# Residual blocks of the last stage in a tile of their own, a regrouped first half of the output projection, and two changed orders at the ends of a two-layer diffusion backbone

## Chip, cores and metric

One core of one Trainium2 chip runs the whole kernel. The metric is the device time of one execution in microseconds; the time of the kernel before is the median of three runs.

## The reference, cut to what matters

The reference is one step of a backbone with two layers on 640 tokens (128 of a prompt, 512 of a sample) of 1024 channels each. What the change touches is the start of the first layer and the second half of the second:

```
m = silu(cond) @ w_mod + b_mod;  shift, scale, gate = split(m, 3)      # both layers
h = rmsnorm(x, norm_g) * (1 + scale) + shift
proj = h @ w_in
...
# odd layer
c_out = b_c * conv3(c_c * x_c) * silu(g_c)
z = conv31(a_d * sigmoid(b_d)) + conv_d_b
z = silu(layernorm(z, ln_g, ln_b));  d_out = z * silu(g_d)
x = x + gate * (concat(c_out, d_out) @ w_out)
# after both layers
y = rmsnorm(x, final_g)
```

## The kernel before, in words

**Layout and arithmetic.** Activations are kept with the channels on the 128 partitions and the 640 tokens in the free dimension, as eight tiles of 128 channels. Every product of the projections is made of three matrix products: weights and activations are each split into a rounded part and the rest (`split`, L111: ScalarE casts the high part, VectorE subtracts for the low part), and hi*hi, hi*lo and lo*hi are added up in PSUM. A weight chunk is 128 by 1024. `dma_w` (L117) loads it into one of two `w_raw` buffers, `split_w` (L122) makes its `w_hi` and `w_lo`, of which there are four each.

**The start** (L264 to L422) is written out by hand: TensorE, ScalarE, VectorE and the DMA queue of SyncE (SP) run in the order of the code. SP loads the eight token tiles `x`, then chunks `wm` of the modulation weights (`load_mod`, L275, two chunks of 512 KB for each of the eight channel tiles, eleven buffers) and the first weight chunks `w_in[20]`, `w_in[21]`, `w_in[22]` (L288 to L291, L358). The third, `w_in[22]`, goes to the buffer that the first chunk has had, so its load waits until VectorE has read the first chunk. TensorE makes the modulation of channel tile d in `mod_rows(d)` (L318, 32 small products on both chunks of d, tile `modacc`), and with `mains(k, ...)` (L364) it multiplies the first three weight chunks with channel tile k as soon as that is normalised. `mains(0, (2,))` (L400) is the first that needs the third chunk.

**The middle** is ordered by the scheduler of the tile framework: the work of an engine is placed by its own estimates, and a pool of buffers that is closed gives its space to the next one, whose tiles then wait for the last use of the old ones. Pool `lp` holds the layer's residual `x2` (eight tiles) and, until the end, the helpers `sq_acc2`, `sq2` and `xr2` of the first layer's closing norm. Pool `lq`, opened at L799, holds what the second layer needs, among it `grow` and `frow`: the gate and the final norm's weights as rows on all partitions, which the SP queue loads there at L810 and L813.

**The last stage** turns the layout: the output projection of the second layer puts tokens on the partitions (five blocks c of 128 tokens) and the 1024 output channels in the free dimension, in two halves of 512 columns. The residual must be turned too. VectorE transposes `x2` in squares of 32 into `xb` (L934, eight transposes, held behind the layer norm by `behind`), and sixteen transfers on the SP queue gather it as `xt` (L937). `xb` and `xt` use the two buffers of tag `h`, which the activations `h_hi` and `h_lo` have held until the last gate's products (`gate_d(3)`, L912). For a finished block of a half, `finish_t` (L952) multiplies PSUM by the gate row into `ft` (L956, which frees the PSUM bank), adds `ft` to `xt` (L957), and squares and sums on ScalarE (L959). In the first half it does so block by block (L977 to L979). In the second half the root of the mean square follows, then the scaling of both halves (ScalarE the left, VectorE the right) and the store of the block.

TensorE's accumulators for the second half partly reuse the banks of the first. Its last 4 of 8 channel tiles go block by block (L993); the last block's columns go in two pieces of 256 (`last`).

Of the kernel before, what the change touches and what calls it, by code (L numbers as in the profile page):

```python
# [57 lines left out]
def build(nc, tc, ctx, a):  # L58
# [18 lines left out]
    def two(t, n):  # L77
        return t.rearrange("p (a b) -> p a b", b=n)
# [189 lines left out]
    with ExitStack() as st:  # L268
# [85 lines left out]
        mod_fin(0, rows)  # L354
        xr(0)
        first = [split_w(raws[0])]
        load_mod(2, 1)
        raws.append(dma_w(w_in[22], nc.sync))  # L358
        load_mod(2, 1)
        load_mod(3)  # L360
        load_mod(4)
        fps = [pmm.tile([P, 1024], F32, name="mm") for _ in range(2)]

# [352 lines left out]
        nc.sync.dma_start(t, a["xN"][:, m])  # L716
        return t

    accs = lp.tile([P, T], F32, name="sq_acc2", bufs=1)

    def finish(m, ps, res, hs_):
        g = mod[0][:, 2, m, :]
        out = x2[m]
        if len(hs_) == 2:
            segs = ((0, ps_prompt(ps), out[:, 256:384], res[:, 256:384]),
                    (1, ps_sample(ps), tok_sample(out), tok_sample(res)))
        elif hs_[0] == 0:
# [9 lines left out]
        sq = lp.tile([P, T], F32, name="sq2", tag="sq2")[:, t0:t1]  # L737
# [58 lines left out]
    GWD = TG + 2 * PADC  # L796
    fill_mod(99)
    modc.close()
    lq = ctx.enter_context(tc.tile_pool(name="lq", bufs=2))  # L799
    dr = ctx.enter_context(tc.tile_pool(name="dr", bufs=1, space=bass.MemoryType.DRAM))  # L800
    gcol = lq.tile([P, 2, SQ], F32, name="gcol", bufs=1)
    grow = lq.tile([P, 2, D], F32, name="grow", bufs=1)
    frow = lq.tile([P, D], F32, name="frow", bufs=1)
# [5 lines left out]
    for c in range(2):  # L809
        nc.sync.dma_start(two(grow[:, c, :], 256), bass.AP(  # L810
            tensor=gd_.tensor, offset=gd_.offset + 256 * c, ap=[[0, P], [SQ * SQ, 4], [1, 256]]))
    fg = a["final_g"]
    nc.sync.dma_start(frow, bass.AP(tensor=fg.tensor, offset=fg.offset, ap=[[0, P], [1, D]]))  # L813
# [100 lines left out]
    for t0, t1 in GH:  # L914
        stat = pst.tile([P, 512], F32, name="stat")
        rs = lp.tile([P, 96], F32, name="rs2")
        bc = pst.tile([P, 512], F32, name="bc")
        stat_add(stat, var[:, t0:t1], t1 - t0, ones, True, True)
        rsqrt_bcast(stat, rs, lambda g, w: bc[:, g * w:(g + 1) * w], t1 - t0, 2.0)
        for i in range(4):  # L920
            ln_last = V.tensor_tensor(cv[i][:, t0:t1], cv[i][:, t0:t1], bc[:, 0:t1 - t0], op=ALU.mult)
    for i in range(4):
        zd = lq.tile([P, TG], F32, name="zd", tag="tmp")
        S.activation(zd, cv[i], AF.Silu, bias=sm("ln_b")[:, i:i + 1], scale=sm("ln_g")[:, i:i + 1])
# [3 lines left out]
        put_o(4 + i, do)  # L928

    NB5 = T // P  # L930
    xb = hpool.tile([P, T // SQ, NK, SQ], F32, name="xb", tag="h", bufs=2)
    xt = hpool.tile([P, NB5, D], F32, name="xt", tag="h", bufs=2)
    for m in range(NK):
        behind(V.transpose(xb[:, :, m, :], two(x2[m], SQ)), ln_last)  # L934
    for q in range(4):
        for g in range(4):
            nc.sync.dma_start(  # L937
# [11 lines left out]
            if pin:  # L949
                tc.keep_in_program_order(op)  # L950

    def finish_t(c, ps, half, n0, n1, j):  # L952
        cond_ = 0 if c == 2 else 1
        cs = slice(512 * half + n0, 512 * half + n1)
        t = lq.tile([P, T], F32, name="ft", tag="tmp")[:, 0:n1 - n0]
        V.tensor_tensor(t, ps[:, n0:n1], grow[:, cond_, cs], op=ALU.mult)  # L956
        V.tensor_tensor(xt[:, c, cs], xt[:, c, cs], t, op=ALU.add)  # L957
        sj = lq.tile([P, 512], F32, name="sqj", tag="c3", bufs=1)
        S.activation(sj[:, 0:n1 - n0], xt[:, c, cs], AF.Square, scale=D ** -0.5, accum_out=sums[:, c, j:j + 1])  # L959
        if j == 0:  # L960
            V.tensor_scalar(sums[:, c, 3:4], sums[:, c, 0:1], EPS, None, op0=ALU.add)
        elif n1 < 512:
            V.tensor_tensor(sums[:, c, 3:4], sums[:, c, 3:4], sums[:, c, j:j + 1], op=ALU.add)
        else:
            S.activation(sums[:, c, j:j + 1], sums[:, c, j:j + 1], AF.Sqrt, bias=sums[:, c, 3:4])
            V.reciprocal(sums[:, c, j:j + 1], sums[:, c, j:j + 1])
            return sums[:, c, j:j + 1]
# [25 lines left out]
    for c in range(NB5):  # L993
        if c < NB5 - 1:
            for k in range(4, NK):
                mm_t(acc[c], ws[k // 2 - 2], c, k, 0, 512, False, k == NK - 1, True)
            r = finish_t(c, acc[c], 1, 0, 512, 1)
        else:
            for j, (ps, n0, n1) in enumerate(last):
                for k in range(4, NK):  # L1000
                    mm_t(ps, ws[k // 2 - 2], c, k, n0, n1, False, k == NK - 1, True)
                r = finish_t(c, ps, 1, n0, n1, 1 + j)
        S.activation(xt[:, c, 0:512], xt[:, c, 0:512], AF.Copy, scale=r)
        V.scalar_tensor_tensor(xt[:, c, 512:D], xt[:, c, 512:D], r, frow[:, 512:D], op0=ALU.mult, op1=ALU.mult)
        if c < NB5 - 1:
            nc.sync.dma_start(a["out_y"][:, c, :], xt[:, c, :])
        else:
            S.dma_start(a["out_y"][:, c, 0:512], xt[:, c, 0:512])
            nc.sync.dma_start(a["out_y"][:, c, 512:D], xt[:, c, 512:D])
# [82 lines left out]
```

## Time and profile before

| what | value |
|---|---|
| median of 3 runs | 592.65 us (592.51 to 593.09) |
| the profiled execution: its own time / its span | 594.55 us / 592.8 us |
| mean granted TensorE clock | 0.992 |
| TensorE matmul (PE) busy | 577.9 us, 97% of the span, 4032 instructions |
| VectorE (DVE) busy | 448.0 us, 76% |
| ScalarE (ACT) busy | 230.2 us, 39% |
| GpSimd (POOL) busy | 39.3 us, 7% |
| DMA | 78.41 MB, mean 132 GB/s |

The profile is of one execution. PE stands for TensorE's matmuls, PEld for its weight loads, DVE for VectorE, ACT for ScalarE, SPq and ACTq for the DMA issues of SyncE and ScalarE. A row of the timeline has the start and the duration in us, the engine, the line of the kernel, the operation, what is written and read, the shape, the count, and in brackets how long the engine sat idle before it and what ended the wait. A row of the stretches has the stretch, its length, busy time and count of PE, PEld, DVE, ACT and POOL, the granted clock, the DMA share and GB/s. A row of the waits says who waited for whom: us in total, times, longest.

### The profile page before, as it was taken

The page shows a single profiled execution, that of the slowest core. Times are in us where ns is not written, and L with a number is a line of the kernel's source. Part 1 is how long each engine was busy: PE and PEld are TensorE (multiplying, and loading weights), DVE is VectorE, ACT ScalarE, POOL GpSimd, SP SyncE. Part 2 cuts the span into 40 slices and gives each one's busy share as a digit, 9 for nine tenths or more (in the row PEclk, how much of TensorE's full clock was granted, in tenths as well). Part 3 has the DMA queues.
Part 4 walks back from the last instruction along what each step waited for, and adds up shares of the span by engine and source line. Part 5 has one row for each costly group of instructions (what it writes and reads, how often), then busy time and mean ns, then how long its engine had stood idle before and what let it go on. Part 6 is the DMA issues. An engine that isn't in the chain of part 4 may idle for free.

```text
span 592.8 us, 10089 instructions
## 1 busy us (share of the span) xinstructions
PE 577.9 (97%) x4032; PEld 527.4 (89%) x4032; DVE 448.0 (76%) x808; ACT 230.2 (39%) x413; POOL 39.3 (7%) x90
## 2 busy tenths in 40 slices
PE   9899999999999999999999999999999999999975
PEld 5689999988988787878999999999999999988764
DVE  0566577699879788765737989999999996369356
ACT  6457322223354555463425531123222222354135
POOL 1000000230005132200000000000000000000000
PEclk9899999999999999999999999999999999999988
DMA  8894666656824242410941232222222222122804
GB/s 315 341 383 139 177 185 174 163 172 228 268 83 145 83 140 76 138 58 28 330 124 37 72 107 72 95 81 76 71 72 72 72 72 74 68 72 65 184 0 179
DMA packets 27823, 78.41 MB, mean 132 GB/s; under 512 B 3200, under 2 KB 8960, under 8 KB 27648
## 3 DMA queue, kind: packets, MB, share of 16 engines
q1 hardware_dynamic: 18416, 43.94, 23.2%
q10 hardware_dynamic: 9360, 33.82, 16.9%
q8 instruction: 32, 0.52, 0.4%
q14 instruction: 15, 0.12, 0.1%
HBM read 71.96 MB, written 3.16 MB: 127 GB/s over the span
## 4 chain that ended last, share of the span: by engine, by line
PE 92%; DMA 3%; DVE 2%; SPq 1%; ACT 1%; issue 1%; POOL 0%; ACTq 0%; DVEq 0%; POOLq 0%
PE mm L162 68%; PE mm L947 5%; PE ps_o L616 3%; PE ps_s L586 3%; PE ps_t L604 3%; PE ps_s L531 2%; PE mm L300 2%; PE modacc L323 1%; DMA w_raw<-in_w_out_odd 1%; DMA wm<-in_w_mod 1%; PE ps_t L531 1%; PE ps_o L531 1%; PE mm L531 1%; SPq L937 1%; PE mm L493 1%; PE bc L200 1%
## 5 line engine op out<-in xcount | busy, mean ns | idle before, releaser
L162 PE MATMUL mm<-h_hi,w_hi 128*128 128x384 f32 (+1 forms) x768 | 181.8, 314 | 0.0
L162 PE MATMUL mm<-h_lo,w_hi 128*128 128x384 f32 (+1 forms) x768 | 181.1, 311 | 0.5 <-DVE h_lo L344 0.5
L162 PE MATMUL mm<-h_hi,w_lo 128*128 128x384 f32 (+1 forms) x768 | 181.2, 311 | 0.0
L112 ACT CAST w_hi<-w_raw 128x1024 fp32r<-128x1024 f32 x68 | 70.9, 1053 | 162.9 <-PE mm L162 132.0
L162 PEld LDWEIGHTS mm<-h_hi,w_hi 128*128 128x128 f32 x768 | 119.4, 189 | 3.5 <-issue 2.1
L162 PEld LDWEIGHTS mm<-h_lo,w_hi 128*128 128x128 f32 x768 | 119.7, 189 | 2.5 <-issue 1.4
L162 PEld LDWEIGHTS mm<-h_hi,w_lo 128*128 128x128 f32 x768 | 119.7, 188 | 1.1 <-issue 1.1
L893 DVE SCALAR_TENSOR_TENSOR cv<-gl,small,cv 128x656 f32<-128x656 f32 x120 | 101.4, 897 | 0.4
L115 DVE TENSOR_TENSOR w_lo<-w_raw,w_hi 128x1024 fp32r<-128x1024 f32 x68 | 83.5, 1229 | 20.2 <-ACT w_hi L112 20.0
L259 DVE SCALAR_TENSOR_TENSOR junk<-wt,condb 128x1024 bf16<-128x1024 f32 x64 | 78.7, 1229 | 4.2 <-DMA wt<-in_w_modT 3.3
L162 PE MATMUL mm<-o_lo,w_hi 128*128 128x384 f32 (+1 forms) x128 | 34.3, 314 | 0.0
L162 PE MATMUL mm<-o_hi,w_lo 128*128 128x256 f32 (+1 forms) x128 | 33.9, 312 | 0.0
L162 PE MATMUL mm<-o_hi,w_hi 128*128 128x384 f32 (+1 forms) x128 | 33.8, 312 | 0.0
L947 PE MATMUL mm<-w_hi,o_hi 128*128 128x512 f32 (+1 forms) x72 | 27.5, 382 | 3.7 <-DVE ft L956 3.7
L947 PE MATMUL mm<-w_lo,o_hi 128*128 128x512 f32 (+1 forms) x72 | 27.1, 376 | 0.0
L947 PE MATMUL mm<-w_hi,o_lo 128*128 128x512 f32 (+1 forms) x72 | 26.8, 372 | 0.0
L606 ACT COPY pt<-ps_t 128x384 f32<-128x384 f32 (+1 forms) x36 | 16.8, 466 | 24.3 <-PE ps_t L604 24.1
L595 ACT ACTIVATE sn<-sn,mx 128x384 f32<-128x384 f32 x32 | 19.6, 614 | 12.6 <-DVE mx L592 11.6
L162 PEld LDWEIGHTS mm<-o_hi,w_hi 128*128 128x128 f32 x128 | 21.6, 188 | 0.8 <-issue 0.6
L162 PEld LDWEIGHTS mm<-o_hi,w_lo 128*128 128x128 f32 x128 | 21.6, 189 | 0.5 <-issue 0.5
L162 PEld LDWEIGHTS mm<-o_lo,w_hi 128*128 128x128 f32 x128 | 21.6, 189 | 0.5 <-issue 0.3
L592 DVE CUSTOM_DVE_ANT_0 sn<-ps_s,bias 128x384 f32<-128x384 f32 x32 | 17.2, 552 | 5.4 <-PE ps_s L586 5.3
(228 smaller groups left out, 712.3 us busy)
## 6 DMA issues: line engine op xcount, KB each, us to landing
wt<-in_w_modT SPq DMA_DIRECT2D x32, 512.0 KB, 4.6
w_raw<-in_w_in_odd ACTq DMA_DIRECT2D x28, 512.0 KB, 4.0
wm<-in_w_mod SPq DMA_DIRECT2D x16, 512.0 KB, 8.1
w_raw<-in_w_in_even ACTq DMA_DIRECT2D x16, 512.0 KB, 3.8
w_raw<-in_w_out_even ACTq DMA_DIRECT2D x8, 512.0 KB
w_raw<-in_w_out_odd ACTq DMA_DIRECT2D x8, 512.0 KB, 4.0
x<-in_xT SPq DMA_DIRECT2D x8, 320.0 KB, 7.0
xre<-in_xN SPq DMA_DIRECT2D x8, 320.0 KB
```

The lines of the kernel that those rows point to most:

```text
L112: op = S.copy(hi, src)
L115: V.tensor_tensor(lo, src, hi.bitcast(F32), op=ALU.subtract)
L162: PE.matmul(ps[:, PB + t0:PB + t1], ww[:, ks], xx[k][:, t0:t1], start=(first and i == 0), stop=(last and i == 2))
L259: tc.keep_in_program_order(V.scalar_tensor_tensor(junk, wt, 1.0, condb[:, c, :], op0=ALU.mult, op1=ALU.mult, accum_out=mod[l][:, j, d, c:c ...
L531: PE.matmul(vps[c], xx[k][:, vsl[c]], ww, start=(k == 0 and n == 0), stop=(k == NK - 1 and n == 2))
L586: chain(PE.matmul(sps[hh][:, 0:384], qq[hr, qs], km, start=(n == 0), stop=(n == 2)))
L592: V.tensor_tensor_reduce(out=sn, in0=sps[:, 0:384], in1=bs[hh][b], scale=-1.0, scalar=3e38, op0=ALU.add, op1=ALU.min, accum_out=mx)
L595: S.activation(sn, sn, AF.Exp, bias=mx, scale=-1.0, accum_out=sume)
L604: chain(PE.transpose(tps[:, c * P:(c + 1) * P], sn[:, c * P:(c + 1) * P], ident))
L616: chain(PE.matmul(po[hr, b * P:(b + 1) * P], vv, pts[hh][:, n * P:(n + 1) * P], start=(n == 0), stop=(n == 2)))
L893: V.scalar_tensor_tensor(z, gl[i][:, w:w + TG], cd[:, i, w:w + 1], z, op0=ALU.mult, op1=ALU.add)
L947: op = PE.matmul(ps[:, n0:n1], xx[k][:, c * P:(c + 1) * P], ww[:, ws], start=(first and i == 0), stop=(last and i == 2))
```

## The change

Five things change; the computation stays the same.

1. In the start, both `wm` chunks of channel tile 2 and both of tile 3 are issued ahead of the third weight chunk `w_in[22]`; before, it stood behind the first `wm` chunk of tile 2.
2. `sq_acc2`, `sq2` and `xr2` move from `lp` to a pool `mid` of their own, which is closed before `lq` is opened, so `lq` lies partly where `mid` was.
3. `xb` gets a buffer of its own in `lq`, and its eight transposes are written right behind the first sum of the layer norm, without `behind`. The buffer of tag `h` that it had goes to `rows`, which holds `grow` and `frow`; their three loads now stand on the SP queue directly ahead of the sixteen `xt` transfers.
4. `finish_t` is cut into `gated` (the product with the gate, which frees the bank), `summed`, `root`, `scaled_a` and `scaled_b`. In the first half all five `gated` come first, each into a buffer of its own, and the five `summed` follow.
5. At the end, the scaling and the store of block 3 are taken apart: its right half is scaled and stored between the last sums, its left half is scaled by ScalarE after the left half of block 4, and stored last, from the ScalarE queue. Both halves of block 4 are stored from the SP queue.

```diff
-        load_mod(2, 1)
+        load_mod(2)
+        load_mod(3)
         raws.append(dma_w(w_in[22], nc.sync))
-        load_mod(2, 1)
-        load_mod(3)
         load_mod(4)
...
-    accs = lp.tile([P, T], F32, name="sq_acc2", bufs=1)
+    midc = ExitStack()
+    mid = midc.enter_context(tc.tile_pool(name="mid", bufs=2))
+    accs = mid.tile([P, T], F32, name="sq_acc2", bufs=1)
...
     modc.close()
+    midc.close()
...
     mu = total("mu", cv)
+    xb = lq.tile([P, T // SQ, NK, SQ], F32, name="xb", bufs=1)
+    for m in range(NK):
+        V.transpose(xb[:, :, m, :], two(x2[m], SQ))
...
-    xb = hpool.tile([P, T // SQ, NK, SQ], F32, name="xb", tag="h", bufs=2)
+    rows = hpool.tile([P, 3, D], F32, name="rows", tag="h", bufs=2)
     xt = hpool.tile([P, NB5, D], F32, name="xt", tag="h", bufs=2)
-    for m in range(NK):
-        behind(V.transpose(xb[:, :, m, :], two(x2[m], SQ)), ln_last)
+    grow, frow = rows[:, 0:2, :], rows[:, 2, :]
...
+    def gated(c, ps, half, n0, n1, tag):
+        t = lq.tile([P, T], F32, name="ft", tag=tag, bufs=2 if tag == "tmp" else 1)[:, 0:n1 - n0]
+        V.tensor_tensor(t, ps[:, n0:n1], grow[:, 0 if c == 2 else 1, 512 * half + n0:512 * half + n1], op=ALU.mult)
+        return t
...
+    fts = [gated(c, acc[c], 0, 0, 512, f"gl{c}" if c < 4 else "pc") for c in range(NB5)]
     for c in range(NB5):
-        finish_t(c, acc[c], 0, 0, 512, 0)
+        summed(c, fts[c], 0, 0, 512, 0)
+        V.tensor_scalar(sums[:, c, 3:4], sums[:, c, 0:1], EPS, None, op0=ALU.add)
         V.tensor_tensor(xt[:, c, 0:512], xt[:, c, 0:512], frow[:, 0:512], op=ALU.mult)
...
+    keep(V.tensor_tensor(sums[:, c, 3:4], sums[:, c, 3:4], sums[:, c, 1:2], op=ALU.add))
+    keep(scaled_b(c - 1, r))
+    nc.sync.dma_start(a["out_y"][:, c - 1, 512:D], xt[:, c - 1, 512:D])
+    rl = root(c, 2)
+    keep(scaled_a(c, rl))
+    keep(scaled_b(c, rl))
+    nc.sync.dma_start(a["out_y"][:, c, 0:512], xt[:, c, 0:512])
+    nc.sync.dma_start(a["out_y"][:, c, 512:D], xt[:, c, 512:D])
+    keep(scaled_a(c - 1, r))
+    S.dma_start(a["out_y"][:, c - 1, 0:512], xt[:, c - 1, 0:512])
```

The SP queue in the start (wm are the modulation chunks, w_raw the third weight chunk of `w_in`); `-` is before, `+` is now:

```order
 L119 DMA w_raw<-in_w_in_even 128x1024
-L278 DMA wm<-in_w_mod 128x1024
+L278 DMA wm<-in_w_mod 128x1024 x4
 L119 DMA w_raw<-in_w_in_even 128x1024
-L278 DMA wm<-in_w_mod 128x1024 x11
-L395 DMA condb<-in_condb 128x2048
+L278 DMA wm<-in_w_mod 128x1024 x8
+L394 DMA condb<-in_condb 128x2048
```

Three modulation chunks have passed the third weight chunk.

VectorE before, at the end of the first half of the output projection (w_lo belongs to weight chunks of the second half, ft is the gated product out of PSUM, xt the turned residual):

```order
L115 TENSOR_TENSOR w_lo<-w_raw,w_hi 128x1024
L956 TENSOR_TENSOR ft<-mm,grow 128x512 x2
L115 TENSOR_TENSOR w_lo<-w_raw,w_hi 128x1024
L957 TENSOR_TENSOR xt<-xt,ft 128x512 x2
L956 TENSOR_TENSOR ft<-mm,grow 128x512
```

And now, at the same place:

```order
L115 TENSOR_TENSOR w_lo<-w_raw,w_hi 128x1024
L956 TENSOR_TENSOR ft<-mm,rows 128x512 x5
L115 TENSOR_TENSOR w_lo<-w_raw,w_hi 128x1024
L961 TENSOR_TENSOR xt<-xt,ft 128x512 x3
L987 TENSOR_SCALAR sums<-sums 128x1
```

Three of the five products that free banks stood behind the first additions to `xt`, and now all five stand ahead of them.

ScalarE at the very end, before (the squares of block 3 and of the two pieces of block 4, the two roots, the two scalings, the store):

```order
L959 ACTIVATE sqj,sums<-xt 128x512
L965 ACTIVATE sums<-sums 128x1
L959 ACTIVATE sqj,sums<-xt 128x256
L1003 ACTIVATE xt<-xt,sums 128x512
L959 ACTIVATE sqj,sums<-xt 128x256
L965 ACTIVATE sums<-sums 128x1
L1003 ACTIVATE xt<-xt,sums 128x512
L1008 DMA out_y<-xt 128x512
```

And now:

```order
L963 ACTIVATE sqj,sums<-xt 128x512
L966 ACTIVATE sums<-sums 128x1
L963 ACTIVATE sqj,sums<-xt 128x256 x2
L966 ACTIVATE sums<-sums 128x1
L971 ACTIVATE xt<-xt,sums 128x512 x2
L1028 DMA out_y<-xt 128x512
```

The scaling of block 3 has moved from between the two pieces of block 4 to behind the scaling of block 4.

More of the change, by code (lines that the diff above doesn't have):

```diff
@@ L736, in finish @@
             return None
-        sq = lp.tile([P, T], F32, name="sq2", tag="sq2")[:, t0:t1]
+        sq = mid.tile([P, T], F32, name="sq2", tag="sq2")[:, t0:t1]
         if m == NK - 1:
@@ L777, in step @@
         def step(k):
-            xr = lp.tile([P, H0], F32, name="xr2")
+            xr = mid.tile([P, H0], F32, name="xr2")
             segs = ((1, 0, 256), (0, 256, 384)) if hf == 0 else ((1, H0, T),)
@@ L801, in build @@
     gcol = lq.tile([P, 2, SQ], F32, name="gcol", bufs=1)
-    grow = lq.tile([P, 2, D], F32, name="grow", bufs=1)
-    frow = lq.tile([P, D], F32, name="frow", bufs=1)
     G.memset(gcol[:, 0, 2 * NK:SQ], 0.0)
@@ L808, in build @@
     nc.sync.dma_start(gd_, gcol[:, 1, :])
[L809 to L813, printed above, removed]
     gl = [lq.tile([P, GWD], F32, name=f"gl{i}", bufs=1) for i in range(4)]
@@ L920, in build @@
         for i in range(4):
-            ln_last = V.tensor_tensor(cv[i][:, t0:t1], cv[i][:, t0:t1], bc[:, 0:t1 - t0], op=ALU.mult)
+            V.tensor_tensor(cv[i][:, t0:t1], cv[i][:, t0:t1], bc[:, 0:t1 - t0], op=ALU.mult)
     for i in range(4):
@@ L930, in build @@
     NB5 = T // P
-    xb = hpool.tile([P, T // SQ, NK, SQ], F32, name="xb", tag="h", bufs=2)
+    rows = hpool.tile([P, 3, D], F32, name="rows", tag="h", bufs=2)
     xt = hpool.tile([P, NB5, D], F32, name="xt", tag="h", bufs=2)
-    for m in range(NK):
-        behind(V.transpose(xb[:, :, m, :], two(x2[m], SQ)), ln_last)
+    grow, frow = rows[:, 0:2, :], rows[:, 2, :]
+    for c in range(2):
+        nc.sync.dma_start(two(grow[:, c, :], 256), bass.AP(
+            tensor=gd_.tensor, offset=gd_.offset + 256 * c, ap=[[0, P], [SQ * SQ, 4], [1, 256]]))
+    fg = a["final_g"]
+    nc.sync.dma_start(frow, bass.AP(tensor=fg.tensor, offset=fg.offset, ap=[[0, P], [1, D]]))
     for q in range(4):
@@ L950, in mm_t, with summed @@
                 tc.keep_in_program_order(op)
-    def finish_t(c, ps, half, n0, n1, j):
-        cond_ = 0 if c == 2 else 1
+    def gated(c, ps, half, n0, n1, tag):
+        t = lq.tile([P, T], F32, name="ft", tag=tag, bufs=2 if tag == "tmp" else 1)[:, 0:n1 - n0]
+        V.tensor_tensor(t, ps[:, n0:n1], grow[:, 0 if c == 2 else 1, 512 * half + n0:512 * half + n1], op=ALU.mult)
+        return t
+    def summed(c, t, half, n0, n1, j):
         cs = slice(512 * half + n0, 512 * half + n1)
-        t = lq.tile([P, T], F32, name="ft", tag="tmp")[:, 0:n1 - n0]
-        V.tensor_tensor(t, ps[:, n0:n1], grow[:, cond_, cs], op=ALU.mult)
         V.tensor_tensor(xt[:, c, cs], xt[:, c, cs], t, op=ALU.add)
@@ L959, in finish_t, with root, scaled_a, scaled_b @@
         S.activation(sj[:, 0:n1 - n0], xt[:, c, cs], AF.Square, scale=D ** -0.5, accum_out=sums[:, c, j:j + 1])
[L960 to L967, printed above, removed]
+    def root(c, j):
+        S.activation(sums[:, c, j:j + 1], sums[:, c, j:j + 1], AF.Sqrt, bias=sums[:, c, 3:4])
+        V.reciprocal(sums[:, c, j:j + 1], sums[:, c, j:j + 1])
+        return sums[:, c, j:j + 1]
+    def scaled_a(c, r):
+        return S.activation(xt[:, c, 0:512], xt[:, c, 0:512], AF.Copy, scale=r)
+    def scaled_b(c, r):
+        return V.scalar_tensor_tensor(xt[:, c, 512:D], xt[:, c, 512:D], r, frow[:, 512:D], op0=ALU.mult, op1=ALU.mult)
     tiles = [pl.tile([P, 1024], F32, name="mm") for _ in range(3)]
@@ L992, in build @@
     ws = [next_w(), next_w()]
[L993 to L1005, printed above, removed]
-            nc.sync.dma_start(a["out_y"][:, c, :], xt[:, c, :])
-        else:
-            S.dma_start(a["out_y"][:, c, 0:512], xt[:, c, 0:512])
-            nc.sync.dma_start(a["out_y"][:, c, 512:D], xt[:, c, 512:D])
+    for c in range(NB5 - 1):
+        for k in range(4, NK):
+            mm_t(acc[c], ws[k // 2 - 2], c, k, 0, 512, False, k == NK - 1, True)
+        summed(c, gated(c, acc[c], 1, 0, 512, "tmp"), 1, 0, 512, 1)
+        if c < NB5 - 2:
+            r = root(c, 1)
+            scaled_a(c, r)
+            scaled_b(c, r)
+            nc.sync.dma_start(a["out_y"][:, c, :], xt[:, c, :])
+    c = NB5 - 1
+    keep = tc.keep_in_program_order
+    for j, (ps, n0, n1) in enumerate(last):
+        for k in range(4, NK):
+            mm_t(ps, ws[k // 2 - 2], c, k, n0, n1, False, k == NK - 1, True)
+        summed(c, gated(c, ps, 1, n0, n1, "tmp"), 1, n0, n1, 1 + j)
+        if j == 0:
+            r = root(c - 1, 1)
+    keep(V.tensor_tensor(sums[:, c, 3:4], sums[:, c, 3:4], sums[:, c, 1:2], op=ALU.add))
[8 more added lines that the diff above has]
+    S.dma_start(a["out_y"][:, c - 1, 0:512], xt[:, c - 1, 0:512])
 def chunks(w):
```

## The prediction

> **What bounds the kernel now.** First the page: its span, and the row of the clock that TensorE was granted.
>
> ```profile
> span 592.8 us, 10089 instructions
> ...
> PEclk9899999999999999999999999999999999999988
> ```
>
> The clock leaves full speed in the second slice and in the last two. Next the waits of TensorE, all that are over 1.5 us:
>
> ```profile
> PE mm L947 <- DVE ft L956: 3.7, 1, 3.7
> PE modacc L323 <- DMA wm<-in_w_mod: 1.9, 1, 1.9
> ```
>
> TensorE works all the time but for two holes: one in the start, for a chunk of modulation weights, and one in the output projection, for a product of VectorE that frees a PSUM bank. The kernel gets shorter where these holes do, or behind TensorE's last product. The stretches around them show what each costs beside the idle time (column PEclk stands ahead of the DMA share):
>
> ```profile
> 23.70:26.80 3.10, 1.24 (x30) 0.97 (x32) 0.83 (x1) 1.61 (x3) 0.00 (x0) 0.96 1.00 399
> 26.80:30.20 3.40, 3.40 (x22) 3.02 (x15) 1.03 (x4) 0.00 (x0) 0.00 (x0) 0.53 1.03 414
> 562.40:566.20 3.80, 0.12 (x1) 0.00 (x0) 3.80 (x10) 1.99 (x6) 0.00 (x0) 0.96 0.00 0
> 566.20:569.50 3.30, 3.28 (x10) 2.75 (x11) 3.05 (x7) 1.53 (x6) 0.00 (x0) 0.53 0.00 0
> ```
>
> Behind each hole stands a stretch of about 3.4 us at a clock of 0.53. TensorE is busy there and does half the work: 3.40 x 0.47 = 1.6 us lost after the first hole, 3.30 x 0.47 = 1.55 us after the second.
>
> **The start.** The timeline shows why the chunk is late:
>
> ```profile
> 11.83 0.33 SPq L278 DMA_DIRECT2D wm<-in_w_mod  x1
> ...
> 18.18 1.22 DVE L115 TENSOR_TENSOR w_lo<-w_raw,w_hi 128x1024 fp32r<-128x1024 f32 x1
> ...
> 19.43 0.33 SPq L119 DMA_DIRECT2D w_raw<-in_w_in_even  x1
> ...
> 23.65 0.41 PE L323 MATMUL modacc<-wm,conds 128*32 128x128 f32 x2
> ...
> 24.27 1.05 ACT L112 CAST w_hi<-w_raw 128x1024 fp32r<-128x1024 f32 x1
> ...
> 25.91 1.36 PE L323 MATMUL modacc<-wm,conds 128*32 128x128 f32 x30 [1.86 <-DMA wm<-in_w_mod]
> ```
>
> SP issues the first chunk of tile 2 at 11.83 and then nothing until 19.43: the third weight chunk needs the buffer of the first, which VectorE reads until 18.18 + 1.22 = 19.40. The second chunk of tile 2 stands behind that, and TensorE gets it at 25.91. The transfers meanwhile run dry:
>
> ```profile
> 13.00:18.80 5.80, 5.49 (x82) 4.07 (x84) 3.03 (x6) 1.94 (x4) 0.00 (x0) 1.00 1.03 408
> 18.80:24.00 5.20, 4.65 (x64) 3.68 (x56) 3.93 (x8) 4.53 (x7) 0.00 (x0) 1.00 0.65 217
> ```
>
> At 217 GB/s instead of 408 for 5.2 us, some 1.0 MB is not moved, two chunks of 0.52 MB. Now three chunks are issued in that pause and are done before they are needed. The removed hole: at the pace of a whole `mod_rows`,
>
> ```profile
> 14.60 1.08 PE L323 MATMUL modacc<-wm,conds 128*32 128x128 f32 x32
> ```
>
> 0.034 us per product, the third would have started at 23.65 + 0.07 = 23.72, not 25.91: 2.2 us, and 1.6 us for the slow stretch, **3.8 us**.
>
> What is late next is the third weight chunk, which three chunks have passed. An earlier load in the full queue, and TensorE's products of weights in the long chain, give its price:
>
> ```profile
> w_raw<-in_w_in_even SPq DMA_DIRECT2D x1, 512.0 KB, 8.8
> ```
> ```profile
> 333.68 180.96 PE mm L162 x1243
> ```
>
> The load row is of the second weight chunk, issued at 11.00 and so landed at 19.8. Behind it now come four `wm` chunks and the third weight chunk, each 0.524 MB / 0.408 = 1.28 us: 19.8 + 5 x 1.28 = 26.2. Bounds: 24.27 (the cast before waited for nothing, so the old landing was no later) and 19.43 + 8.8 = 28.2. From 26.2, the cast takes 1.05 and the low part 1.22: ready at 28.5. TensorE comes to it after two `mod_rows` (1.08 each), two `mains` of six products (180.96 / 1243 = 0.146, so 0.87 each) and a small product of 0.3: 23.65 + 4.2 = 27.85, and needs the low part two pairs later, at 28.4. I take 0.1 us of wait, with 0 and 2.1 (from 28.2) as ends. ScalarE's and VectorE's next normalised tile stands behind that cast and follows about 2 us ahead of its use.
>
> **The hole at 562.** VectorE and TensorE there, with the release in the chain of waits:
>
> ```profile
> 551.83 1.28 DVE L956 TENSOR_TENSOR ft<-mm,grow 128x512 f32<-128x512 f32 x2
> ...
> 561.74 1.29 DVE L957 TENSOR_TENSOR xt<-xt,ft 128x512 f32<-128x512 f32 x2 [6.25 <-DMA xt<-xb]
> ...
> 562.24 0.28 PE L947 MATMUL mm<-w_hi,o_lo 128*128 128x256 f32 x1
> ...
> 565.48 1.28 DVE L956 TENSOR_TENSOR ft<-mm,grow 128x512 f32<-128x512 f32 x2
> ```
> ```profile
> 546.41 6.69 DMA w_raw<-in_w_out_odd
> ...
> 558.03 3.69 DMA xt<-xb
> ...
> 566.22 8.57 PE mm L947 x36
> 574.79 2.72 PE stat L947 x12
> ```
>
> VectorE frees the banks of blocks 0 and 1 and then waits in the addition until the last transfer of `xt` has landed. Blocks 2 and 3 are queued behind it; block 3 is read from 565.48 and TensorE goes on at 566.22. A product of 512 columns takes 2.72 / 12 = 0.227 us, one of 256 half of that, so the next would have started at 562.24 + 0.11 = 562.35: 3.85 us of hole, plus 1.55, is **5.4 us**.
>
> Now the five products that free banks stand ahead of any addition: 5 x 0.64 = 3.2 us from 551.8 at the latest. TensorE, done with the first half at 551.8, has three blocks of new products in free banks (9 x 0.227 = 2.0 us) before it needs the banks of blocks 0 and 1 (free after 1.3 us), and 0.7 us later those of blocks 2 and 3 (free after 2.6). No hole is left by this sum. The additions still wait for `xt`, but behind them TensorE needs VectorE only at the end of the first block of the second half:
>
> ```profile
> 523.50 0.70 ACT L883 ACTIVATE gd<-mm 128x640 f32<-128x640 f32 x1
> ...
> 542.75 15.89 SPq L937 DMA_DIRECT2D xt<-xb  x16
> ...
> 574.83 0.69 DVE L956 TENSOR_TENSOR ft<-mm,grow 128x512 f32<-128x512 f32 x1 [4.45 <-PE mm L947]
> ```
>
> 574.83 less 5.4 is 569.4, and five additions of 0.64 with as many scalings of that size take 6.5 us, so `xt` may land as late as 562 and cost nothing. It will be earlier: the buffers of tag `h` are free when the last gate is read at 523.5, and the transposes are done by then, so the three loads of `rows` (1.5 MB) and the sixteen transfers start there and not at 542.75. With the 15.9 us of issuing, 3.7 for the last landing (the chain's row) and 7 for `rows` (1.5 MB at the poor 217 GB/s), they end near 550.
>
> **The transposes** are moved into a stretch in which VectorE is nearly full:
>
> ```profile
> L934 DVE STREAM_TRANSPOSE xb<-x 128x640 f32<-128x640 f32 x8 | 6.4, 823 | 0.0
> ```
> ```profile
> 400.00:500.00 100.00, 100.00 (x684) 100.00 (x683) 96.83 (x122) 25.74 (x29) 0.49 (x9) 1.00 0.22 75
> 500.00:516.00 16.00, 16.00 (x109) 15.83 (x108) 3.23 (x4) 4.93 (x7) 0.00 (x0) 1.00 0.20 67
> ```
>
> I cost them at nothing: 6.4 us of backlog runs off in the 16 - 3.2 = 12.8 us that VectorE idles between 500 and 516, and until then TensorE has three accumulators, so a tile that is freed up to one weight chunk late (48 x 0.146 = 7.0 us) holds nobody up. Without that cover it would be up to 6.4 us. The pool `mid`, the five buffers and the split of `finish_t` add no operation.
>
> **The end.** Rows from the last addition on, and the GB/s from 585 to 593 in slices of 0.2 us:
>
> ```profile
> 586.60 0.43 DVE L957 TENSOR_TENSOR xt<-xt,ft 128x256 f32<-128x256 f32 x1
> 586.67 0.72 ACT L1003 ACTIVATE xt<-xt,sums 128x512 f32<-128x512 f32 x1
> ...
> 587.30 0.40 ACT L959 ACTIVATE sqj<-xt 128x256 f32<-128x256 f32 x1
> ...
> 588.38 0.72 ACT L1003 ACTIVATE xt<-xt,sums 128x512 f32<-128x512 f32 x1 [0.23 <-DVE sums L966]
> ...
> 589.13 0.38 ACTq L1008 DMA_DIRECT2D out_y<-xt  x1
> 589.16 0.33 SPq L1009 DMA_DIRECT2D out_y<-xt  x1
> ```
> ```profile
> GB/s 471 389 430 369 348 0 0 0 0 0 0 0 0 0 0 0 0 20 451 410 410 369 451 410 103 358 358 379 410 379 359 348 31 0 0 0 0 0 0 0
> ```
>
> The last square starts at 587.30, when the scaling of block 3 is over, though its addition ends at 587.03: without that scaling in between it starts 0.23 us earlier. Against that, three stores of 256 KB now follow the last root instead of two. The left half of block 3 is scaled after that of block 4 and goes last. The last two stores moved from 590.0 to 591.4, 1.4 us for 512 KB, so 768 KB take 2.1 us: +0.7. Together **+0.45 us**, with -0.2 (the third store hides) and +0.9 as ends.
>
> **The sum.** -3.8 + 0.1 - 5.4 + 0.45 = -8.65 us. The profiled execution took 594.55 (its span 592.8 and 1.75 around it), so 585.9; it lay 1.9 over the median of 592.65, so the median becomes **584.0**. The bounds of the main case: the raw chunk 0 to 0.8, the end -0.2 to +0.9, either hole give or take 0.3: 582.8 to 585.2.
>
> **The rivals.**
>
> *The third weight chunk becomes the wait* (0.07). It lands at 28.2, TensorE stands 2.1 us and pays a slow stretch of 1.6: 3.7 - 0.1 given back, 587.6. For it: the load that took 8.8. Against: the same queue moved 408 GB/s without a pause.
>
> *The slow stretch of the start stays* (0.06). It may hang on the thin work of that time and not on the 2.2 us hole alone: 584.0 + 1.6 = 585.6. Against: it begins right behind the hole, as the other does. [...]
>
> *The freeing products are held up themselves* (0.08). Ahead of all five stands `w_lo` of a chunk of the second half. Its cast (1.05) and itself (1.22) must end by 552.5, so its load must land by 550.2; the load row of 6.69 us shows how slow one is beside `xt`. If it lands 6 us later, the hole is back: 589.4. Against: it is issued earlier now, since VectorE has no transposes between.
>
> *Both of these* (0.03): 584.0 + 3.6 + 5.4 = 593.0, no change.
>
> *Slower* (0.03): VectorE becomes the bound between 345 and 500. If the transposes push the tiles it frees more than 7.0 us behind TensorE, their 6.4 us show as holes, and with two slow stretches of 1.6 cost 9.6: 593.6. For it: 96.83 of 100 us busy. Against: the 12.8 idle us behind.
>
> **Chances.** The likeliest case has 0.73. A measurement of this kernel tells about 0.2%, 1.2 us, from no change. Faster by more than that are the main case and the first three rivals: 0.94; the same 0.03, slower 0.03. The range of 582.8 to 587.6 holds the main case, the slow stretch and most of the first rival, and leaves out some 0.15.
>
> **What would show it.** Right: no wait of TensorE over 1 us, and full clock from the start to its last product; the third weight chunk's cast near 26.2; the five gated products in one row, then the additions; `xt` landed before 556; about 0.5 us more from the last product to the end of the span. Wrong: a wait of TensorE at L162 for `w_hi` near 28, a slow slice there without a hole, a hole near 550, or waits for VectorE between 340 and 500.

## The result, and the profile after

| what | before | after |
|---|---|---|
| median | 592.87 us (592.51 to 594.58, 4 runs) | 586.62 us (586.35 to 587.18, 4 runs) |
| ratio | | 0.989, 95% interval 0.987 to 0.9911 |
| profiled execution, its time / its span | 594.55 / 592.8 us | 586.67 / 584.9 us |
| mean granted clock in it | 0.992 | 0.998 |

The kernel is 6.25 us faster by the medians and 7.9 us by the two profiled executions; 8.65 was forecast for both. The time of 586.62 lies 2.6 us above the forecast of 584.0. It is inside the range of 582.8 to 587.6, but above the 585.2 at which the main case ended. The page of the profile after has no slice at a lower clock:

```profile
span 584.9 us, 10092 instructions
...
PEclk9999999999999999999999999999999999999999
```

Both long waits of TensorE are gone. The longest wait of all is now one at the very start, which was there before too; the only one for a modulation chunk is new (us in total, times, longest):

```profile
PE mm L300 <- POOL ones L86: 1.3, 1, 1.3
PE modacc L323 <- DMA wm<-in_w_mod: 0.6, 1, 0.6
```

**The start.** TensorE's modulation of tiles 1 to 4, ScalarE's cast of the third weight chunk and its first gate (line L223), which I take as the end of the start:

```profile
19.08 1.07 PE L323 MATMUL modacc<-wm,conds 128*32 128x128 f32 x30 [0.61 <-DMA wm<-in_w_mod]
...
24.10 1.08 PE L323 MATMUL modacc<-wm,conds 128*32 128x128 f32 x32
...
27.30 1.08 PE L323 MATMUL modacc<-wm,conds 128*32 128x128 f32 x32
...
30.85 1.08 PE L323 MATMUL modacc<-wm,conds 128*32 128x128 f32 x32
```
```profile
26.89 1.05 ACT L112 CAST w_hi<-w_raw 128x1024 fp32r<-128x1024 f32 x1 [2.04 <-DMA w_raw<-in_w_in_even]
```
```profile
51.46 1.29 ACT L223 ACTIVATE gb<-mm 128x640 f32<-128x640 f32 x2
```

Before, tiles 3 and 4 and the first gate stood at:

```profile
30.63 1.08 PE L323 MATMUL modacc<-wm,conds 128*32 128x128 f32 x32
...
33.83 1.08 PE L323 MATMUL modacc<-wm,conds 128*32 128x128 f32 x32
```
```profile
54.44 1.29 ACT L223 ACTIVATE gb<-mm 128x640 f32<-128x640 f32 x2
```

Tile 2 runs in one piece without a wait. But tile 1, for which the profile before lists no wait, now waits 0.61 us for its second chunk. The third weight chunk is there at 26.89 (forecast 26.2, bounds to 28.2).

**The output projection.** VectorE at the end of the first half, and at the first block of the second:

```profile
547.92 3.25 DVE L956 TENSOR_TENSOR ft<-mm,rows 128x512 f32<-128x512 f32 x5 [2.45 <-PE mm L949]
551.16 1.23 DVE L115 TENSOR_TENSOR w_lo<-w_raw,w_hi 128x1024 fp32r<-128x1024 f32 x1
552.95 1.90 DVE L961 TENSOR_TENSOR xt<-xt,ft 128x512 f32<-128x512 f32 x3 [0.56 <-DMA xt<-xb]
...
566.54 0.69 DVE L956 TENSOR_TENSOR ft<-mm,rows 128x512 f32<-128x512 f32 x1 [6.74 <-PE mm L949]
```

Five products in one row, then the additions, released by `xt` at 552.95 where it was 561.74. The sixteen transfers of `xt` were issued from 521.21 on:

```profile
521.21 29.40 SPq L939 DMA_DIRECT2D xt<-xb  x16
```

VectorE waits 6.74 us for TensorE ahead of the second half's first block, where it was 4.45. TensorE is busy in all of this stretch (18.00 of 18.00 us, 14.30 before):

```profile
552.00:570.00 18.00, 18.00 (x92) 15.29 (x92) 9.08 (x20) 5.57 (x13) 0.00 (x0) 1.00 0.04 7
```

**The end.** TensorE's last product, VectorE's reading of it (with the reading in the profile before below it), the two last scalings on ScalarE and the store behind them:

```profile
577.54 0.28 PE L949 MATMUL mm<-w_hi,o_lo 128*128 128x256 f32 x1
```
```profile
577.85 0.42 DVE L956 TENSOR_TENSOR ft<-mm,rows 128x256 f32<-128x256 f32 x1 [0.27 <-PE mm L949]
```
```profile
586.14 0.42 DVE L956 TENSOR_TENSOR ft<-mm,grow 128x256 f32<-128x256 f32 x1 [0.26 <-PE mm L947]
```
```profile
579.90 1.33 ACT L971 ACTIVATE xt<-xt,sums 128x512 f32<-128x512 f32 x2 [0.23 <-DVE sums L967]
581.26 0.35 ACTq L1028 DMA_DIRECT2D out_y<-xt  x1
```

VectorE reads that product at 577.85, and the span ends 7.05 us later. Before, it was 586.14, and the span ended 6.66 us later.

Against the profile of before the sum closes: the first gate stands 54.44 - 51.46 = 2.98 us earlier, VectorE's reading of the last product 586.14 - 577.85 = 8.29, of which 5.31 belong to the projection, and the end takes 0.4 back: 7.9. The medians show 1.65 us less. That is what the experiments are about.

### The profile page after: what moved, and what is told of

Same layout as the page of the kernel before. It is cut to its first block, busy times and chain, and to the rows that moved or that the text cites. A ratio compares the mean times of both kernels' runs of the same rounds, so it can differ in the third digit from the quotient of the medians.

```text
span 584.9 us, 10092 instructions
## 1 busy us (share of the span) xinstructions
PE 574.5 (98%) x4032; PEld 524.6 (90%) x4032; DVE 447.5 (77%) x808; ACT 230.4 (39%) x413; POOL 37.8 (6%) x90
## 4 chain that ended last, share of the span: by engine, by line
PE 96%; DMA 1%; DVE 1%; ACT 1%; issue 0%; POOL 0%; ACTq 0%; POOLq 0%
PE mm L162 68%; PE mm L949 8%; PE ps_o L615 3%; PE ps_s L585 3%; PE ps_t L603 3%; PE ps_s L530 2%; PE mm L300 2%; DMA w_raw<-in_w_in_even 1%; PE ps_t L530 1%; PE stat L949 1%; PE ps_o L530 1%; PE bc L949 1%; PE mm L530 1%; PE modacc L323 1%; PE mm L492 1%; PE bc L200 1%
```

## Experiments

**Theory A:** the slow stretch behind the start's hole comes in some executions of the kernel before only, and the profiled one was such. Its 1.6 us and the one long wait are most of what this execution lay above the median, so the start is worth about 1 us in most executions. **Theory B:** the stretch comes in every execution, the start is worth 3 us, and the 1.9 us between profile and median lie elsewhere.

### The parts one by one

The kernel before, unchanged:

> The kernel before, unchanged, to see what its own executions differ by. Theory A (the slow stretch of 1.6 us behind the 2.2-us hole of the start comes in some executions only, and the profiled one of before had it): its executions fall into two groups, some near 594.5 us with a mean clock near 0.992, most near 592.6 with a clock near 0.995; a profile of the second kind has the hole of the start but no stretch at 0.53 behind it. Theory B (the stretch always comes, and the 1.9 us by which the profiled execution lay above the median have nothing to do with the clock): all executions have a mean clock near 0.992, whatever their time, and each profile has both stretches.

592.57 us (591.23 to 594.14, 12 executions), ratio 1.0 (0.9987 to 1.0013). Its profiled execution took 592.28 us, at a clock of 0.995. The start of this one, with the first gate, the hole of the projection and VectorE's reading of the last product:

```profile
18.28 0.38 PE L323 MATMUL modacc<-wm,conds 128*32 128x128 f32 x2 [0.44 <-DMA wm<-in_w_mod]
19.47 1.07 PE L323 MATMUL modacc<-wm,conds 128*32 128x128 f32 x30 [0.81 <-DMA wm<-in_w_mod]
...
25.37 1.07 PE L323 MATMUL modacc<-wm,conds 128*32 128x128 f32 x30 [0.48 <-DMA wm<-in_w_mod]
```
```profile
52.36 1.29 ACT L223 ACTIVATE gb<-mm 128x640 f32<-128x640 f32 x2
```
```profile
25.40:28.80 3.40, 3.40 (x53) 3.01 (x57) 1.48 (x6) 0.78 (x1) 0.00 (x0) 1.00 1.00 400
560.20:563.78 3.58, 0.20 (x2) 0.00 (x0) 3.58 (x9) 1.84 (x6) 0.00 (x0) 1.00 0.00 0
563.78:567.20 3.42, 3.42 (x10) 2.84 (x11) 3.17 (x8) 1.61 (x6) 0.00 (x0) 0.50 0.00 0
```
```profile
583.87 0.42 DVE L956 TENSOR_TENSOR ft<-mm,grow 128x256 f32<-128x256 f32 x1 [0.26 <-PE mm L947]
```

The same program waits 1.73 us for its chunks, about as much as in the first profile (1.86), but in three pieces, two of them ahead of tile 1. The clock behind the last piece is 1.00, and the start is 2.1 us earlier (52.36 for 54.44). The hole of the projection and its half clock are there as before. Theory A holds for this execution. But the twelve do not fall into A's two groups: none is near 594.5 us at 0.992. Six have a clock of 0.995 or 0.996, five have 0.993, and one took 591.23 us at 0.998. By an estimate from the rows above, one slow stretch of 3.4 us at 0.50 takes 0.003 off the mean over 590 us (3.42 x 0.50 / 590), so this last one can hardly have had any. Of 51 other executions of this kernel, timed beside the runs of this section, seven have a clock of 0.992 or less and took 594.8 to 597.5 us; these have no trace.

The order of the start alone:

```diff
-        load_mod(2, 1)
+        load_mod(2)
+        load_mod(3)
         raws.append(dma_w(w_in[22], nc.sync))
-        load_mod(2, 1)
-        load_mod(3)
         load_mod(4)
```

> Only the order of the start is changed (part 1); homes, grouping and end are those of before. Theory A: TensorE is 3 us ahead of the profiled execution of before behind the start, but most executions of before had only 1.3 to 1.4 us of it to lose, so the median falls by 1.3, to about 591.4 us. Theory B: 3.0 us in every execution, 589.7 us. Both: the hole of 3.9 us near 560 and its slow stretch stay.

592.11 us (590.79 to 593.84), ratio 0.999 (0.9979 to 1.0002): at most 1.2 us faster, 0.5 by the medians, less than either theory had, and B is excluded. Its profile has a wait of 0.32 us ahead of tile 1 and the first gate at 51.63, 0.73 ahead of the kernel before in the profile above.

The change with the old start (the same edit the other way round):

> The changed kernel with the old order of the start (part 1 undone). Theory A (most executions have no slow stretch in the start, and the waits of the start are 1.7 us in three pieces of which 0.9 go): 0.9 us slower than the changed kernel at the median, 587.5 us, with single executions 1.6 us above that at a clock of 0.995 instead of 0.998. Theory B (3.0 in every execution): 589.6 us.

588.04 us (587.69 to 590.36), ratio 0.9911 (0.9878 to 0.9943), against 586.62 and 0.989 with the new start: 1.2 to 1.4 us, nearer to A than to B. The slowest of its executions, 590.36 us, is the one with the profile, and shows the stretch again (the tile-2 wait, and the time from behind the hole on):

```profile
26.59 1.41 PE L323 MATMUL modacc<-wm,conds 128*32 128x128 f32 x30 [2.50 <-DMA wm<-in_w_mod]
```
```profile
26.60:28.00 1.40, 1.40 (x31) 1.00 (x31) 0.00 (x0) 0.00 (x0) 0.00 (x0) 0.71 1.03 421
28.00:31.40 3.40, 3.40 (x18) 3.21 (x22) 1.50 (x5) 0.12 (x1) 0.00 (x0) 0.62 1.02 418
31.40:34.00 2.60, 2.60 (x43) 2.40 (x44) 2.52 (x4) 1.81 (x3) 0.00 (x0) 1.00 1.04 414
```

No wait at tile 1, one of 2.50 us at tile 2, then half clock for 3.4 us (an estimate, taking the clock as either 1.00 or the 0.50 of the row 563.78:567.20 above: 1.40 x 0.29 / 0.5 + 3.40 x 0.38 / 0.5), and the first gate at 55.13. All starts in the old and the new order of which there is a profile, those of the kernels below too (waits in us, the pieces of one tile added up):

| order of the start | kernels | waits at tile 1 | at tile 2 | half clock behind | first gate |
|---|---|---|---|---|---|
| old | before; change with the old start | 0; 0 | 1.86; 2.50 | yes | 54.44; 55.13 |
| old | before again; grouping, order held; homes; grouping, old order | 1.25; 0.68; 1.36; 0.81 | 0.48; 1.31; 0.33; 0.77 | no | 52.36; 52.60; 52.19; 52.17 |
| new | change; start alone; old end; GpSimd at the end; holes of 3, 4, 5 | 0.61; 0.32; 1.26; 0.80; 0.67, 1.06, 0.18 | 0 | no | 51.46; 51.63; 51.65; 51.31; 51.10, 51.72, 51.32 |

So the old start comes in two kinds. Three kernels have the old start and no hole at the end (homes, grouping in the old order, change with the old start): of their 18 executions two have a clock of 0.995 or less and took 590.4 and 590.6 us, the other 16 have 0.996 to 0.998 and took 586.9 to 589.1. Those without a trace are put down to a kind by their clock alone.

The first half's evictions grouped, nothing else changed; the last line holds VectorE's order in the second half, which the scheduler would set otherwise:

```diff
+    fts = [gated(c, acc[c], 0, 0, 512, f"gl{c}" if c < 4 else "pc") for c in range(NB5)]
     for c in range(NB5):
-        finish_t(c, acc[c], 0, 0, 512, 0)
+        finish_t(c, acc[c], 0, 0, 512, 0, fts[c])
...
+            behind(op, scales[c - 2] if c >= 2 else half_done)
```

> Only the grouping of the first half's evictions (part 4, first half) in the kernel before, with VectorE's order in the second half held to that of before; xb, grow and frow have their old homes, so xt still lands near 561.5 us. If the order of VectorE is what made the hole: the hole and its slow stretch go, -5.3 us, 587.4, since the five additions and scalings behind xt are done at about 568.2, ahead of the end of the second half's first block at about 569.4. If the late xt is what made it: the end waits for the additions, and at most 2 us are gained, 590.7 or more.

589.86 us (589.57 to 590.95), ratio 0.9958 (0.9941 to 0.9974), between the two. The long hole is gone although `xt` comes at 559.71; two waits of TensorE of 0.8 us together are left, and most of the rest that is lost lies in VectorE's order at the end:

```profile
559.71 1.90 DVE L963 TENSOR_TENSOR xt<-xt,ft 128x512 f32<-128x512 f32 x3 [5.50 <-DMA xt<-xb]
...
580.44 0.75 DVE L1012 SCALAR_TENSOR_TENSOR xt<-xt,sums,frow 128x512 f32<-128x512 f32 x1
581.39 0.16 DVE L969 TENSOR_TENSOR sums<-sums 128x1 f32<-128x1 f32 x1 [0.20 <-ACT sqj L965]
581.47 0.42 DVE L954 TENSOR_TENSOR ft<-mm,grow 128x256 f32<-128x256 f32 x1
```

TensorE's last product ends at 579.94, but VectorE reads it at 581.47, behind the scaling of block 3 and the sums: 1.5 us late.

The same with each row of VectorE in the order of before (the second half's operations written out in that order and kept so):

```diff
+        if half:
+            keep(op)
+            if c == 0:
+                behind(op, half_done)
```

> Grouping alone once more (old homes, old start, old end), now with every row of VectorE in the second half in the order of before and the gated product of its first block held behind the first half's additions. The grouping with a held order gave 2.8 us, and its profile put 1.4 us of late scalings and 0.8 us of waits against it. If those are all that grouping lacks: the hole and its slow stretch are gone and 5.0 to 5.3 us are gained, 587.4 us, as much as the homes alone gave (4.9) or a little more. If an xt that lands at 559.7 costs something of itself: 588.5 us or more.

588.22 us (587.54 to 588.73), ratio 0.9907 (0.9873 to 0.9941): 5.0 us by the medians. The time lies between the two forecasts and its interval holds both, so the profile decides: the additions start at 559.28 (559.31 in the kernel before again), TensorE's one wait in the projection is 0.33 us, and the span ends 6.6 us behind the reading of the last product, as before. Grouping alone takes the hole away but for that wait, with `xt` as late as it was.

The homes alone: `mid`, `xb` and `rows` as in the change, but the evictions block by block, old start, old end.

```diff
-    fts = [gated(c, acc[c], 0, 0, 512, f"gl{c}" if c < 4 else "pc") for c in range(NB5)]
     for c in range(NB5):
-        summed(c, fts[c], 0, 0, 512, 0)
-        V.tensor_scalar(sums[:, c, 3:4], sums[:, c, 0:1], EPS, None, op0=ALU.add)
+        finish_t(c, acc[c], 0, 0, 512, 0)
```

> Only the homes (parts 2 and 3): xt lands near 555 us instead of 561.7, but the evictions go block by block as before. If the late xt alone made the hole: the product of block 3, which frees the bank that TensorE needs near 562.3, is done near 559, no hole is left and 5.3 us are gained, 587.4 us; then either half of the tail's change would have done. If the order of VectorE is needed too: a hole of 1 to 2 us is left, with a slow stretch or without, 589 to 591 us.

587.68 us (586.86 to 590.61), ratio 0.9922 (0.9901 to 0.9943). The additions start at 556.35, and of the hole is left:

```profile
560.83 0.39 PE L950 MATMUL mm<-w_hi,o_hi 128*128 128x256 f32 x1 [0.58 <-DVE ft L957]
```

So either half of the tail's change takes 4.9 to 5.0 us by the medians, and by the waits that are left the other adds 0.3 to 0.6 us. With both, TensorE does not wait there at all.

### The end, and the start once more

The change with the old end (`finish_t`, the scalings and stores in the order of before):

> The changed kernel with the old end (part 5 undone). By the profiles the span from TensorE's last product to its end was 6.66 us before and 7.1 now: with the old end 0.4 us less, 586.2 us where the changed kernel has 586.6, and the last store is that of block 4, from the ScalarE queue. If the stores do not set the end: within 0.1 of the changed kernel.

586.2 us (585.64 to 586.48), ratio 0.9871 (0.984 to 0.9901). In its profile VectorE reads the last product at 578.03 and the span ends at 584.7: 6.67 us for 7.05, as expected. The intervals of the two ratios overlap; the medians say the same as the profiles, 0.4 us. It has the lowest median of all versions here.

The old end, and the third weight chunk ahead of tile 3's modulation chunks:

```diff
         load_mod(2)
-        load_mod(3)
         raws.append(dma_w(w_in[22], nc.sync))
+        load_mod(3)
         load_mod(4)
```

> The changed kernel with the old end, and with the third raw chunk issued ahead of tile 3's two modulation chunks instead of behind them. The third chunk then lands about 2.5 us earlier, near 24.3, and TensorE does not wait for its low part (0.3 us now); tile 3's chunks land near 26.9, just ahead of their use near 27.0. Expected: 0.3 us less than with the old end alone, 585.9 us; if tile 3's chunks become the wait, as much as the old end alone or more, 586.2 to 586.6.

586.41 us (586.22 to 586.71), ratio 0.9875 (0.9845 to 0.9906): no difference. The cast starts at 25.10, where it was 26.89 in the change, and tile 3 does not wait either, but only 0.17 us came of it (tile 4 at 30.88, 31.05 with the old end alone): the third chunk was not more than about 0.3 us late in these traces (tile 3 to tile 4 takes 3.55 us in the change, 3.20 before).

The old end, with the left half of block 3 scaled by GpSimd:

```diff
-        S.activation(xt[:, c, 0:512], xt[:, c, 0:512], AF.Copy, scale=r)
+        if c == NB5 - 2:
+            G.tensor_scalar(xt[:, c, 0:512], xt[:, c, 0:512], r, None, op0=ALU.mult)
+        else:
+            S.activation(xt[:, c, 0:512], xt[:, c, 0:512], AF.Copy, scale=r)
```

> The changed kernel with the old end, but the left half of block 3 scaled on GpSimd, which is idle there, instead of on ScalarE between the two pieces of block 4. ScalarE's last square then starts 0.23 us earlier, as in the change, and block 3 is stored whole ahead of block 4, as before. If GpSimd takes under 2 us for 128x512: 0.2 us less than the old end alone, 586.0 us. It takes 1.0 us for 128x128 of this kind elsewhere in the kernel; at that rate 4 us, so that block 3's store comes last, about 583.5 plus 2 us of landing: 1 us more, 587.2 us.

586.94 us (586.72 to 587.54), ratio 0.9904 (0.9891 to 0.9917): not faster. GpSimd took 1.67 us, within the first case, yet the end takes 7.2 us (577.68 to 584.9), 0.55 more than with the old end alone. VectorE's scaling of the other half, at the same time, accounts for most of it. With the old end alone the same scaling was:

```profile
578.83 0.74 DVE L1022 SCALAR_TENSOR_TENSOR xt<-xt,sums,rows 128x512 f32<-128x512 f32 x1
```

Now:

```profile
578.33 1.67 POOL L1022 TENSOR_SCALAR xt<-xt,sums 128x512 f32<-128x512 f32 x1 [124.82 <-DVE sums L967]
```
```profile
578.48 1.18 DVE L1025 SCALAR_TENSOR_TENSOR xt<-xt,sums,rows 128x512 f32<-128x512 f32 x1
579.58 0.15 DVE L981 TENSOR_TENSOR sums<-sums 128x1 f32<-128x1 f32 x1
...
580.35 0.75 DVE L1025 SCALAR_TENSOR_TENSOR xt<-xt,sums,rows 128x512 f32<-128x512 f32 x1
```

It took 1.18 us beside GpSimd and 0.74 without it (0.75 for the other block), and the sum for the last root stands behind it: 0.44 of the 0.55 us. So the square's 0.2 us bring nothing. This is one trace; no run slows VectorE there by other means.

### How long a hole draws the half clock

To make holes to size: old end, evictions block by block, new start, and additional products of VectorE whose result nobody reads (the output stays as it is):

```diff
+        if c == 1:
+            for _ in range(3):
+                late = V.tensor_tensor(junk, xt[:, c, 0:512], frow[:, 0:512], op=ALU.mult)
...
+        if c == 2:
+            behind(gates[2], late)
```

> A hole in TensorE made to size: the changed kernel with the old end, the first half's evictions block by block again, and three additional products of VectorE (128x512, a column of the residual times the weights row into a tile that nobody reads, about 0.63 us each) between the additions of blocks 0 and 1 and the product of block 2. With the homes alone TensorE waited 0.6 us there, so the hole should be 1 to 2 us. Theory A (a slow stretch of about 3.4 us at half clock follows a hole from some length between 1.3 and 1.9 us on, as the profiles so far have it): none or seldom, 587.2 to 588.2 us at a clock of 0.997. [...]

> The same with four additional products: a hole of 1.7 to 2.6 us. Theory A: a slow stretch in most executions, so 2 us of hole and 1.6 us of stretch above the old end alone, 589.5 to 590.4 us at 0.995. [...]

> The same with five additional products: a hole of 2.3 to 3.2 us. Theory A: a slow stretch in every execution, 590.1 to 591.0 us at 0.995. [...]

With three: 589.75 us (586.68 to 590.85), ratio 0.9942 (0.9922 to 0.9962); with four: 589.41 (587.06 to 590.93), 0.995 (0.9934 to 0.9967); with five: 591.63 (587.32 to 593.25, twelve executions), 0.9956 (0.9934 to 0.9978). The size of the hole was not under control: `xt` releases the additions at 554.67, 552.91 and 555.62 in the three profiles, so their holes are 1.98, 0.25 and 4.10 us; the execution with the last is the slowest of its twelve. By these measured sizes, the stretch behind the hole of 1.98 (with three), and those behind the hole of 4.10 (with five):

```profile
561.14 0.38 PE L949 MATMUL mm<-w_hi,o_hi 128*128 128x256 f32 x1 [1.98 <-DVE ft L958]
```
```profile
561.14:562.50 1.36, 1.36 (x7) 1.36 (x8) 1.36 (x4) 0.16 (x2) 0.00 (x0) 0.68 0.00 0
562.50:566.00 3.50, 3.50 (x13) 2.79 (x13) 2.55 (x6) 1.45 (x4) 0.00 (x0) 0.64 0.00 0
566.00:567.00 1.00, 1.00 (x8) 0.87 (x8) 0.00 (x0) 0.00 (x0) 0.00 (x0) 1.00 0.00 0
```
```profile
563.53 0.58 PE L949 MATMUL mm<-w_hi,o_hi 128*128 128x256 f32 x1 [4.10 <-DVE ft L958]
```
```profile
559.00:563.50 4.50, 0.43 (x4) 0.23 (x2) 4.43 (x8) 0.53 (x1) 0.00 (x0) 0.92 0.00 0
563.50:567.00 3.50, 3.46 (x10) 2.89 (x11) 3.25 (x8) 1.64 (x6) 0.00 (x0) 0.50 0.00 0
567.00:570.40 3.40, 3.40 (x15) 2.97 (x14) 0.70 (x2) 0.00 (x0) 0.00 (x0) 0.61 0.00 0
```

None of the three runs went as theory A forecast it. With three products most times lie above the forecast: in the trace the hole was at its upper end and did draw the stretch, and four of six executions have a clock of 0.995 or 0.996. With four and five it came less often than forecast (three of six at 0.995 or less, nine of twelve above 590 us), which fits holes that early transfers made short, but of executions without a trace the hole isn't known. By the same estimate, a hole of 1.98 us was followed by 3.4 us at half clock (1.36 x 0.32 / 0.5 + 3.50 x 0.36 / 0.5), a hole of 4.10 us by 6.9 us: 0.7 in the first row, 3.5 in the second, 2.65 in the third. The second is twice the first. In all profiles here, single waits of up to 1.31 us were followed by no such stretch, those of 1.86, 1.98, 2.50, 3.39, 3.44 and 3.70 us by one, and that of 4.10 by two. This fits A of these three runs, a stretch from some length between 1.3 and 1.9 us on; that none follows a hole of 1.98 or of 4.10 us is excluded by the rows above.

## Why the prediction was right or wrong

**The range** held, and in part by luck. The likeliest case had bounds of 582.8 to 585.2, and 586.62 lies above them. The stretch from 585.2 to 587.6 was put into the range for two rivals, and neither of them came.

**The mechanism** was right in the main, and the signs came as named: tile 2 without a wait, five gated products in one row, `xt` ahead of 556, full clock to the last product, a third weight chunk at 26.89 for 26.2, the end 0.4 us longer for 0.45. The waits that would have shown it wrong are not there. That `xt` came near the forecast of 550 is luck in part: its sixteen issues took 29.40 us, not 15.9, while they began at 521.21, earlier than 523.5 plus 7 for `rows`.

**The hole of the projection**: 5.4 forecast; 5.31 between the profiles, 5.1 against the kernel before again (583.87 - 577.85 less the 0.90 of the start). Right in size. But the prediction named two parts for it, early `xt` and grouped products. The runs show that each nearly does it alone (waits of 0.58 and 0.33 us are left). The additions behind a late `xt` were done ahead of TensorE's next need, as the prediction worked out itself (`xt` "may land as late as 562"); it did not ask whether the homes were then needed at all.

**The start** has the term that was wrong: "**3.8 us**", 2.2 for the hole and 1.6 for the stretch. Between the two profiles these 3.8 were there. Tile 2 begins 0.45 us later than before (24.10 for 23.65) and tile 3 begins 3.33 us earlier (27.30 for 30.63), which makes 3.78. But the 0.45 were lost ahead of tile 2, where tile 1 now waits, and the sum has no term for that. From tile 3 to tile 4 another 0.35 were lost, since the third chunk's low part comes about 0.3 us late (0.1 forecast). So 2.98 were left. Between ordinary executions it gave 0.9 (52.36 to 51.46), and 0.5 to 1.4 by the medians. The half clock of the start belonged to a rarer kind of execution, and that is where the term fails.

From that follows the error of the sum: "it lay 1.9 over the median of 592.65, so the median becomes 584.0". The 1.9 us were taken off the changed kernel as well, as if they lay outside the change. They lay in the start's one long wait and its stretch, which the change removes: beside the second profile of the same kernel, the first gate came 2.08 us later. So they were counted twice, and that is 1.9 of the 2.6 us by which the median was missed. The profiled execution was missed by 0.8 (585.9 forecast, 586.67 measured). With the start at 0.9, the hole at 5.1 and the end at 0.4 the sum is 592.65 - 5.6 = 587.05; measured 586.62.

**The transposes** cost nothing, as forecast: TensorE has no wait for VectorE between 340 and 512 in the profile after. **The end** cost 0.4 us, as forecast, and by both of its terms: the last scalings start 0.19 us earlier behind VectorE's reading of the last product (2.05 for 2.24; 0.23 forecast), and from there to the end of the span it takes 0.58 longer (5.00 for 4.42; 0.7 forecast).

**The rivals.** None came. Of the second ("the slow stretch of the start stays") the question was put wrongly: it stays or goes per execution. A stretch of about 3.4 us at half clock stood behind single holes of 1.86 us (the kernel before), 1.98 us (three additional products) and 2.50 us (the change with the old start).

**Open.** Why the waits of the old start fall at tile 1 in most executions and in one piece at tile 2 in others is not settled; their sum is 1.6 to 2.5 us in either. Also, the start alone leaves 5 of 12 executions at a clock of 0.993, as many as the kernel before has, and lower than one stretch makes. So in kernels with the hole of the projection a clock of 0.993 does not tell that the start had its stretch, and where the rest lies can't be told without their traces. That hole and stretch of the projection vary too is likely (one execution of the kernel before had 0.998) but not shown. Last, whether the length of a single hole draws the half clock, or the share of idle time in a stretch of a few us, is not told apart, and no trace has a hole between 1.31 and 1.86 us.

## What to carry to other kernels

A stretch at lower clock in one profile is not yet a cost of the kernel: look at the clock and time of several executions before it goes into the sum, and when a profiled execution lies above the median, first ask whether the edit removes what made it so. When a wait can be removed by two means (free the bank earlier, or bring the data earlier), try each alone. Here a long wait of TensorE with a stretch at half clock behind it cost about 1.7 us more than its length (3.42 us at 0.50), while the short waits for the same transfers cost no more than their own length: 1.73 us of them became 0.61, and the first gate came 0.90 us earlier (52.36 to 51.46).

## What the runs showed of the hardware

Behind single holes of TensorE of 1.86, 1.98 and 2.50 us (the kernel before, three additional products, the change with the old start) its granted clock was 0.50 for about 3.4 us, by the estimate above, and behind one of 4.10 us (five additional products) for about 6.9 us. Behind one of 3.39 us (the kernel before again) a row of 3.42 us shows 0.50. Single waits of 1.31 us and less were followed by no such stretch: behind the 1.31 us of the grouping with its order held the clock was 1.00.

```profile
25.60:29.00 3.40, 3.40 (x52) 3.01 (x56) 1.35 (x5) 0.00 (x0) 0.00 (x0) 1.00 1.03 419
```

Between 1.31 and 1.86 us no trace has a hole.

The landing of `xt` moved by 2.7 us between executions of nearly the same program: it released the additions at 552.95 in the change, at 554.30 with GpSimd at the end, and at 554.67, 552.91 and 555.62 with three, four and five additional products, one trace of each.

VectorE's 128x512 scaling took 1.18 us beside GpSimd's scaling of 1.67 us, and 0.74 to 0.75 without it.
